# A lower scheduler priority for the position sums and splits of the compressed inputs, in a two-layer hybrid decoder trunk

## The chip, the cores and the metric

The kernel runs on one core of one Trainium2 chip. The metric is the device time of one execution in microseconds (us); the smaller, the better. The core has a TensorE for matmuls (PE in the profile, its weight loads PEld), a VectorE (DVE), a ScalarE (ACT), a GpSimd (POOL) and a SyncE (SP), which here only issues transfers. Each engine works through its own list of instructions in the order in which they were put there, and waits where an operand or a buffer isn't ready.

## The reference: what is computed

Two layers. In each, h = RMSNorm(x) is multiplied by one wide projection W_in. Its columns feed three mixers: a conformer convolution (31 taps, depthwise), a native sparse attention (NSA) with compressed, selected and window branches, and a latent attention (MLA) with four heads. Then come cross attention and a SwiGLU feed-forward. The change stands where the NSA's compressed keys and values are made:

```python
def compress_blocks(tok, pos, w1, b1, w2, n_cmp):
    idx = CMP_STRIDE * jnp.arange(n_cmp)[:, None] + jnp.arange(CMP_BLOCK)[None, :]
    blk = tok[:, idx] + pos[:, None, :]
    blk = blk.transpose(0, 1, 3, 2, 4).reshape(bsz, n_cmp, NSA_KV_GROUPS, CMP_BLOCK * NSA_HEAD_DIM)
    return jax.nn.gelu(blk @ w1 + b1) @ w2
```

There are 31 windows of 32 tokens, stride 16, in two groups of heads, once for the keys (i = 0) and once for the values (i = 1). Everything is 512 tokens by 1024 channels in float32.

## The kernel before

A matrix product in float32 is made from three products of a faster type: each operand is split into a high and a low part, hi = cast(x) on ACT and lo = x - hi on DVE (`hilo`, L93 and L94), and `mm3` (L86, L87, L88) adds hi*hi, lo*hi and hi*lo in a bank of PSUM. So nearly every matrix that PE reads has first passed ACT and DVE.

The instructions aren't listed by hand. The program runs under a scheduler with a modelled clock, which at each point gives an engine the ready instruction with the lowest priority number; that number (`tc.cur_priority`) counts up in the order of the code. A larger number means: later, if anything else is ready. The result is a fixed list for each engine, so on the chip nothing can overtake. The taps of the convolution (`ca`, L587, 120 operations per layer) are written with 100000 added to the number, and fill DVE where nothing else is ready.

The change stands in `mix`, in which the four MLA heads (`head_scores`: scores in `ps_s`, L843 to L847, and the softmax, L852 to L856; `head_mix`: transposes of the probabilities into `ps_t`, L865, their split into `PTh` and `PTl`, then three products a block into `ps_pv`, L878 to L882, and at a head's end the split of the sum, `om`) are interleaved with a filler, `work()`, that takes the other projections step by step. The filler's order in that stretch is: the projection of the compressed keys' input with `windows(p, 0)`; a part of the convolution; two stacked keys interleaved with `compress_in(0)`; the projection of the values' input with `windows(p, 1)`; the first step of `compress_out(0)`; the projection of two query heads (`stacked_queries`); the second step of `compress_out(0)`; and so on with the values, for which `compress_in(1)` reads what `windows(p, 1)` has made.

`windows(p, i)` takes the bank p of the projection. For each of two groups g it adds the position to the even and the odd tokens (L649, two operations of 64x496 from PSUM into `xf`), and splits the sums into `xt` (two casts on ACT and two subtractions on DVE, of 128x248 each). Later `compress_in` uses `xt` as weights of PE (L697, L698).

`compress_out(i)` adds the bias (L705), adds the two halves of the product (L706), and forms the GELU (L707, L708, the tanh on ACT in L709, L710) in a tile `h1`; PE then transposes it (L714). `xf` and `h1` share the tag `gB`, which has one buffer (`bufs` 1). So the first write of `h1` for the keys, L705, can only be made when `xf` of `windows(p, 1)` has been read to the end, by the last two subtractions into `xt`. The tag `ps_t` has two banks, `ps_pv` one, `PTh` and `PTl` have two buffers each, `raw` (weights as loaded) two of 1 MB.

All of this occurs once per layer: `windows(p, 0)` at 97 us and `windows(p, 1)` at 151 us in layer 0, and again in layer 1, where `xf` of `windows(p, 1)` stands at 1089 us.

## Time and profile before

| What | Value |
|---|---|
| Median of 3 runs | 1899.36 us (1898.75 to 1899.78) |
| Profiled execution, its own time | 1898.13 us |
| Its span in the trace | 1896.4 us |
| Granted TensorE clock, mean | 0.999 |
| PE busy | 1877.0 us (99%) |
| DVE busy | 1509.8 us (80%) |
| ACT busy | 1045.7 us (55%) |
| POOL busy | 269.6 us (14%) |
| The four `windows`: L649, 16 operations | 672 ns each |
| Their casts on ACT, 16 | 400 ns each |
| Their subtractions on DVE, 16 | 410 ns each |

The profiled execution is 1.23 us below the median, and its span 1.73 us below its time. A row of a timeline gives the start, the length, the engine, the line, the operation, and the tiles it writes and reads; a bracket at the end is the idle time just before it and what ended that. Rows of one engine overlap a little, since an instruction starts while the one ahead is still writing, so the distance of two starts is what an instruction costs. Matmuls are shown at 0.39 us for 512 columns, and follow each other at 0.23 us.

### The profile page before, as it was taken

What the parts mean: (1) busy time and instruction counts of PE and PEld (TensorE: products, weight loads), DVE (VectorE), ACT (ScalarE), POOL (GpSimd) and SP (SyncE); (2) the same over time, 40 slices, a digit from 0 to 9 for tenths busy, and PEclk for the clock granted to TensorE, in tenths of its full rate; (3) what the DMA queues carried; (4) which work ended last, traced back from release to release, by engine and by line L of the source; (5) the groups of instructions that cost most, each with busy time, mean ns of one, the idle gap of its engine ahead of it and who ended that gap; (6) DMA issues with size and microseconds to landing.
All of it is one profiled execution on the core that took longest, in us unless ns stands there. A gap on an engine that the chain in (4) does not pass through costs nothing.

```text
span 1896.4 us, 29494 instructions
## 1 busy us (share of the span) xinstructions
PE 1877.0 (99%) x10988; PEld 1643.5 (87%) x10988; DVE 1509.8 (80%) x2754; ACT 1045.7 (55%) x1952; POOL 269.6 (14%) x433
## 2 busy tenths in 40 slices
PE   9999999999999999999999999999999999999998
PEld 8887888888887999998888878888888879999986
DVE  7999898764466899998869999986645678999886
ACT  5366557763355645456543765676633465454564
POOL 1211111111122211100022111111112221110000
PEclk9999999999999999999999999999999999999999
DMA  6666554455866666656566665435566766766664
GB/s 188 164 155 185 143 129 127 123 147 157 238 180 161 187 163 186 185 181 197 180 181 164 163 197 129 127 100 136 157 182 177 216 165 159 202 164 163 209 191 159
DMA packets 217644, 318.52 MB, mean 168 GB/s; under 512 B 16352, under 2 KB 153843, under 8 KB 217500
## 3 DMA queue, kind: packets, MB, share of 16 engines
q1 hardware_dynamic: 183116, 216.39, 35.9%
q0 software_dynamic: 31872, 94.39, 23.9%
q10 hardware_dynamic: 2512, 5.85, 0.8%
q8 instruction: 86, 1.41, 0.3%
q14 instruction: 58, 0.48, 0.1%
HBM read 307.13 MB, written 97.54 MB: 213 GB/s over the span
## 4 chain that ended last, share of the span: by engine, by line
PE 87%; DVE 5%; issue 4%; ACT 2%; DMA 1%; POOL 1%; POOLq 0%; SPq 0%; DVEq 0%; ACTq 0%
PE ps_mm L86 14%; PE ps_mm L88 14%; PE ps_mm L87 14%; PE ps_s L86 3%; PE ps_s L88 3%; PE ps_s L87 3%; PE ps_t L86 2%; PE ps_t L87 2%; PE ps_t L88 2%; PE ps_t L1083 2%; PE ps_pv L86 1%; PE ps_pv L88 1%; PE ps_pv L87 1%; PE ps_mm L1374 1%; PE ps_mm L1373 1%
## 5 line engine op out<-in xcount | busy, mean ns | idle before, releaser
L93 ACT CAST wh<-raw 128x1024 fp32r<-128x1024 f32 (+3 forms) x419 | 422.8, 1012 | 498.0 <-PE ps_mm L87 123.5
L94 DVE TENSOR_TENSOR wl<-raw,wh 128x1024 fp32r<-128x1024 f32 (+3 forms) x419 | 488.6, 1172 | 221.6 <-ACT wh L93 218.4
L86 PE MATMUL ps_mm<-hTh,wh 128*128 128x512 f32 (+1 forms) x1152 | 414.6, 360 | 0.5 <-DVE kc L94 0.5
L87 PE MATMUL ps_mm<-hTl,wh 128*128 128x512 f32 (+1 forms) x1152 | 411.2, 357 | 0.0
L88 PE MATMUL ps_mm<-hTh,wl 128*128 128x512 f32 (+1 forms) x1152 | 410.5, 357 | 0.5 <-DVE wl L94 0.5
L88 PEld LDWEIGHTS ps_mm<-hTh,wl 128*128 128x128 f32 x1152 | 217.8, 189 | 32.7 <-DVE wl L94 1.3
L86 PEld LDWEIGHTS ps_mm<-hTh,wh 128*128 128x128 f32 x1152 | 217.9, 189 | 29.4 <-issue 1.3
L87 PEld LDWEIGHTS ps_mm<-hTl,wh 128*128 128x128 f32 x1152 | 217.9, 189 | 26.3 <-issue 0.7
L587 DVE SCALAR_TENSOR_TENSOR ca<-u,vT,ca 128x512 f32<-128x512 f32 x240 | 177.5, 747 | 2.9
L466 POOL DMA_DIRECT2D up<-in_w_gate_up_dram x128 | 85.0, 664 | 538.6 <-PE ps_mm L88 380.9
L466 POOL DMA_DIRECT2D down<-in_w_down_dram x132 | 85.3, 646 | 478.6 <-PE ps_mm L88 255.2
L93 ACT CAST PTh<-ps_t 128x512 fp32r<-128x512 f32 (+4 forms) x136 | 70.6, 519 | 53.2 <-PE ps_t L1083 39.6
L1046 ACT ACTIVATE P<-P,ss 128x512 f32<-128x512 f32 (+3 forms) x128 | 71.6, 560 | 49.2 <-DVE ss L1043 48.2
L86 PE MATMUL ps_s<-rh,wh 128*128 128x256 f32 x320 | 90.6, 283 | 0.0
L87 PE MATMUL ps_s<-rl,wh 128*128 128x256 f32 x320 | 90.6, 283 | 0.0
L88 PE MATMUL ps_s<-rh,wl 128*128 128x256 f32 x320 | 90.6, 283 | 0.0
L94 DVE TENSOR_TENSOR PTl<-ps_t,PTh 128x512 fp32r<-128x512 f32 (+2 forms) x120 | 71.6, 598 | 9.0 <-ACT PTh L93 7.9
L1054 ACT ACTIVATE P<-P,sr 128x512 f32<-128x512 f32 (+3 forms) x128 | 63.3, 555 | 16.9 <-DVE sr L1052 16.8
L86 PE MATMUL ps_mm<-op,wh 128*128 128x512 f32 (+1 forms) x192 | 68.8, 359 | 0.0
L88 PE MATMUL ps_mm<-op,wl 128*128 128x512 f32 (+1 forms) x192 | 68.4, 356 | 0.3
L87 PE MATMUL ps_mm<-op,wh 128*128 128x512 f32 (+1 forms) x192 | 68.0, 355 | 0.0
L86 PEld LDWEIGHTS ps_s<-rh,wh 128*128 128x128 f32 x320 | 61.4, 192 | 0.0
(567 smaller groups left out, 4652.0 us busy)
## 6 DMA issues: line engine op xcount, KB each, us to landing
up<-in_w_gate_up_dram POOLq DMA_DIRECT2D x128, 320.0 KB, 4.4
down<-in_w_down_dram POOLq DMA_DIRECT2D x132, 256.0 KB, 4.3
raw<-in_w_in_dram SPq DMA_DIRECT2D x32, 1024.0 KB
raw<-in_w_gate_up_dram SPq DMA_DIRECT2D x60, 512.0 KB
raw<-up SPq DMA_DIRECT2D x40, 512.0 KB
raw<-down SPq DMA_DIRECT2D x40, 512.0 KB
raw<-in_w_down_dram SPq DMA_DIRECT2D x30, 512.0 KB
raw<-in_w_in_dram SPq DMA_DIRECT2D x26, 512.0 KB
```

The lines of the kernel that those rows point to most:

```text
L86: nc.tensor.matmul(o, lh, rh, start=start, stop=False)
L87: nc.tensor.matmul(o, lh, rl, start=False, stop=False)
L88: tick(nc.tensor.matmul(o, ll, rh, start=False, stop=stop))
L93: nc.scalar.copy(hi, src)
L94: nc.vector.tensor_tensor(lo, src, f(hi), op=OP.subtract)
L466: d = nc.gpsimd.dma_start(dst, src, accum_op=op) if op else nc.gpsimd.dma_start(dst, src)
L587: nc.vector.scalar_tensor_tensor(c, u[:, j:j + T], cw[:, m, j:j + 1], c, op0=OP.mult, op1=OP.add)
L1046: nc.scalar.activation(p[:, c], p[:, c], AF.Exp, bias=s[:, k:k + 1], scale=-1.0, accum_out=s[:, 4 + k:5 + k])
L1054: nc.scalar.activation(P[k], P[k], AF.Copy, scale=r[:, k:k + 1])
L1083: nc.tensor.transpose(tp[:, w:w + 128], P[k][:, j * 128:(j + 1) * 128], ident)
L1373: nc.tensor.matmul(accs[t], xh, u[0][:, k, :], start=j == 0, stop=False)
L1374: nc.tensor.matmul(accs[t], xh, u[1][:, k, :], start=False, stop=False)
```

## The change

Around the loop over the groups in `windows`, the priority number is raised by 50000 and then lowered again:

```diff
             xf = new("gB", (128, 2, 512), name="xf")
+            tc.cur_priority += 50000
             for g in range(2):
                 xv = xf[:, g, 0:496].rearrange("p (k c) -> p k c", k=16)
...
                 for k in range(2):
                     hilo(xt[k][:, :, 0, c], xt[k][:, :, 1, c], xv[:, 8 * k:8 * k + 8])
+            tc.cur_priority -= 50000
             X[i] = xt
```

The adds of L649, the casts and the subtractions into `xt` thus come behind whatever else is ready, and ahead of the taps alone. No operation is added or taken away. Two lines are added, so L649 is L650 in the changed kernel, and lines from L654 on are two higher (L705 is L707, L714 is L716, L881 is L883).

DVE in layer 0 at `windows(p, 1)` before, from the last-but-one subtraction into `xt` (`P` and `s1` belong to the softmax of a head, `wl` to the weights of the next projection, `w1` to the weights of `compress_in(1)`, `op` to stacked operands):

```order
L94 TENSOR_TENSOR xt_1628<-xf_1631,xt_1628 128x8x31
L852 ISA P_1681,s1_1682<-ps_s_1675,mask_823,rst_908 128x256
L852 ISA s1_1682 128x1
L705 TENSOR_TENSOR h1_1644<-ps_mm_1342,b1_1343 62x256
L94 TENSOR_TENSOR wl_1727<-raw_1652,wh_1726 128x1024
L706 TENSOR_TENSOR h1_1644<-h1_1644,ps_mm_1342 62x256
L855 RECIPROCAL s1_1682<-s1_1682 128x1
L94 TENSOR_TENSOR w1_1760<-raw_1761,w1_1760 128x512
L707 TENSOR_TENSOR h1_1644<-h1_1644 62x256
L410 SCALAR_TENSOR_TENSOR op_1706<-ps_mm_1651,op_1706 64x512
L708 SCALAR_TENSOR_TENSOR h1_1644<-h1_1644 62x256
L94 TENSOR_TENSOR PTl_1740<-ps_t_1734,PTh_1739 128x512
```

In this list L705 comes right behind the subtractions, and L710 two rows below this piece.

The same engine and place in the changed kernel, from the last subtractions into `xt` on:

```order
L94 TENSOR_TENSOR xt_1627<-xf_1631,xt_1627 128x8x31
L94 TENSOR_TENSOR om_1806<-ps_pv_1613,om_1805 128x512
L94 TENSOR_TENSOR PTl_1860<-ps_t_1856,PTh_1859 128x256
L94 TENSOR_TENSOR xt_1628<-xf_1631,xt_1628 128x8x31
L587 SCALAR_TENSOR_TENSOR ca_1302<-u_1297,vT_301,ca_1302 128x512
L707 TENSOR_TENSOR h1_1644<-ps_mm_1342,b1_1343 62x256
L94 TENSOR_TENSOR PTl_1911<-ps_t_1906,PTh_1910 128x384
L708 TENSOR_TENSOR h1_1644<-h1_1644,ps_mm_1342 62x256
L94 TENSOR_TENSOR PTl_1982<-ps_t_1976,PTh_1981 128x512
L709 TENSOR_TENSOR h1_1644<-h1_1644 62x256
L587 SCALAR_TENSOR_TENSOR ca_1302<-u_1297,vT_301,ca_1302 128x512
L710 SCALAR_TENSOR_TENSOR h1_1644<-h1_1644 62x256
```

The subtractions into `xt`, and L705 (now L707) with them, have moved behind the split `om_1806` at the end of one head and the first split of the next head (`PTl_1860`); the chain of `h1` is now interleaved with two more of those splits and with taps. L710 (now L712) follows two rows below.

PE in the same place before, from the last products of that head (`pv_1613`) to the projection of the query heads (`ps_mm_1725`):

```order
L846 MATMUL ps_s_1790<-op_590,op_1073 128x512
L847 MATMUL ps_s_1790<-op_591,op_1073 128x512
L880 MATMUL ps_pv_1613<-PTh_1739,op_1147 128x512
L881 MATMUL ps_pv_1613<-PTl_1740,op_1147 128x512
L882 MATMUL ps_pv_1613<-PTh_1739,op_1148 128x512
L714 MATMUL ps_mm_1712<-ident_81,h1_1644 128x62 x2
L86 MATMUL ps_mm_1725<-hTh_135,wh_1726 128x512
L87 MATMUL ps_mm_1725<-hTl_136,wh_1726 128x512
L88 MATMUL ps_mm_1725<-hTh_135,wl_1727 128x512
```

And in the changed kernel, from the last transposes of the next head's first round on:

```order
L867 MATMUL ps_t_1976<-ident_81,P_1607 128x128
L867 MATMUL ps_t_1976<-ident_81,P_1681 128x128
L867 MATMUL ps_t_1976<-ident_81,P_1607 128x128
L867 MATMUL ps_t_1976<-ident_81,P_1541 128x128
L882 MATMUL ps_pv_1875<-PTh_1910,op_1158 128x384
L883 MATMUL ps_pv_1875<-PTl_1911,op_1158 128x384
L884 MATMUL ps_pv_1875<-PTh_1910,op_1159 128x384
L882 MATMUL ps_pv_1875<-PTh_1981,op_1147 128x512
L883 MATMUL ps_pv_1875<-PTl_1982,op_1147 128x512
L884 MATMUL ps_pv_1875<-PTh_1981,op_1148 128x512
L716 MATMUL ps_mm_1712<-ident_81,h1_1644 128x62 x2
L86 MATMUL ps_mm_1725<-hTh_135,wh_1726 128x512
```

The transposes L714 (now L716) have moved behind 26 instructions of the next head (`ps_t_1856`, `ps_s_1863`, `ps_t_1906`, `ps_t_1976` and all products of `ps_pv_1875`); no matmul of a projection stands among those. The same 26 are moved in layer 1.

DVE at `windows(p, 0)` in layer 0 before (`kf` and `op` of MLA's keys and rotary queries):

```order
L410 SCALAR_TENSOR_TENSOR op_1042<-ps_t_1034,op_1042 64x512
L649 TENSOR_TENSOR xf_1082<-ps_mm_928,vT_301 64x496 x2
L94 TENSOR_TENSOR op_1060<-kf_1061,op_1059 128x512
L410 SCALAR_TENSOR_TENSOR op_1070<-ps_t_1065,op_1070 64x512
L94 TENSOR_TENSOR xt_1079<-xf_1082,xt_1079 128x8x31 x2
L649 TENSOR_TENSOR xf_1082<-ps_mm_928,vT_301 64x496 x2
L410 SCALAR_TENSOR_TENSOR op_1073<-ps_t_1065,op_1073 64x512
L94 TENSOR_TENSOR xt_1079<-xf_1082,xt_1079 128x8x31 x2
L94 TENSOR_TENSOR wl_1099<-raw_1095,wh_1098 128x1024
```

And now:

```order
L410 SCALAR_TENSOR_TENSOR op_1042<-ps_t_1034,op_1042 64x512
L650 TENSOR_TENSOR xf_1082<-ps_mm_928,vT_301 64x496
L94 TENSOR_TENSOR wl_1099<-raw_1095,wh_1098 128x1024
L94 TENSOR_TENSOR op_1060<-kf_1061,op_1059 128x512
L410 SCALAR_TENSOR_TENSOR op_1070<-ps_t_1065,op_1070 64x512
L816 TENSOR_TENSOR kf_1116<-ps_pv_1106,rk_997 128x512
L650 TENSOR_TENSOR xf_1082<-ps_mm_928,vT_301 64x496
L410 SCALAR_TENSOR_TENSOR op_1073<-ps_t_1065,op_1073 64x512
L94 TENSOR_TENSOR op_1115<-kf_1116,op_1114 128x512
```

Here one add of L649 (now L650) has stayed, the second stands five rows later, and the splits into `xt` come behind this piece.

## Prediction

> **What bounds the kernel now.** I read the page's busy times, its slices and its chain first, then PE's waits, then the timeline of DVE and PE where the moved work stands.

> ```profile
> span 1896.4 us, 29494 instructions
> PE 1877.0 (99%) x10988; PEld 1643.5 (87%) x10988; DVE 1509.8 (80%) x2754; ACT 1045.7 (55%) x1952; POOL 269.6 (14%) x433
> PEclk9999999999999999999999999999999999999999
> PE 87%; DVE 5%; issue 4%; ACT 2%; DMA 1%; POOL 1%; POOLq 0%; SPq 0%; DVEq 0%; ACTq 0%
> ```

> PE is busy for 99% of the span at the full clock, and holds 87% of the chain that ended last. No operation is added or removed, so time can only come from PE's waits, and only go into new ones. The waits of PE that touch the moved work are few (engine, line waited at, what it waits for, total, times, longest):

> ```profile
> PE ps_pv L881 <- DVE PTl L94: 2.4, 2, 1.2
> PE ps_mm L714 <- DVE h L710: 0.9, 2, 0.4
> PE ps_mm L86 <- DVE kc L94: 0.5, 2, 0.3
> PE ps_t L86 <- DVE op L410: 0.4, 1, 0.4
> ```

> The first two occur once per layer each, at `windows(p, 1)`; the last once, at `windows(p, 0)` of layer 0. This is DVE there in layer 0:

> ```profile
> 150.75 2.05 DVE L649 TENSOR_TENSOR xf<-ps_mm,vT 64x496 f32<-64x496 f32 x3
> 152.72 0.73 DVE L94 TENSOR_TENSOR xt<-xf,xt 128x248 fp32r<-128x248 f32 x2
> 153.47 0.68 DVE L649 TENSOR_TENSOR xf<-ps_mm,vT 64x496 f32<-64x496 f32 x1
> 154.18 0.56 DVE L94 TENSOR_TENSOR PTl<-ps_t,PTh 128x384 fp32r<-128x384 f32 x1
> 154.65 0.73 DVE L94 TENSOR_TENSOR xt<-xf,xt 128x248 fp32r<-128x248 f32 x2
> ...
> 155.71 0.41 DVE L705 TENSOR_TENSOR h<-ps_mm,b 62x256 f32<-62x256 f32 x1
> 156.04 1.21 DVE L94 TENSOR_TENSOR wl<-raw,wh 128x1024 fp32r<-128x1024 f32 x1
> 157.28 0.42 DVE L706 TENSOR_TENSOR h<-h,ps_mm 62x256 f32<-62x256 f32 x1
> ...
> 159.79 0.68 DVE L94 TENSOR_TENSOR PTl<-ps_t,PTh 128x512 fp32r<-128x512 f32 x1
> 160.50 0.69 DVE L410 SCALAR_TENSOR_TENSOR op<-ps_mm,op 64x512 fp32r<-64x512 f32 x1
> 161.22 0.42 DVE L710 SCALAR_TENSOR_TENSOR h<-h 62x256 f32<-62x256 f32 x1
> 161.67 0.35 DVE L852 CUSTOM_DVE_ANT_0 P<-ps_s,mask,rst 128x128 f32<-128x128 f32 x1
> ...
> 161.95 0.69 DVE L94 TENSOR_TENSOR w<-raw,w 128x512 fp32r<-128x512 f32 x1
> 162.55 0.28 DVE L94 TENSOR_TENSOR PTl<-ps_t,PTh 128x128 fp32r<-128x128 f32 x1
> ...
> 163.67 0.69 DVE L94 TENSOR_TENSOR om<-ps_pv,om 128x512 fp32r<-128x512 f32 x1
> 164.27 1.22 DVE L94 TENSOR_TENSOR wl<-raw,wh 128x1024 fp32r<-128x1024 f32 x1
> 165.41 0.16 DVE L855 RECIPROCAL s<-s 128x1 f32<-128x1 f32 x1
> ...
> 167.84 2.32 DVE L587 SCALAR_TENSOR_TENSOR ca<-u,vT,ca 128x512 f32<-128x512 f32 x3
> ...
> 172.21 0.42 DVE L94 TENSOR_TENSOR PTl<-ps_t,PTh 128x256 fp32r<-128x256 f32 x1
> ```

> The reader is to see that DVE is without a gap (no row has a bracket with idle time) from 150.75 to 161.64, where L710 ends: here DVE sets the pace. PE shows the same from its side:

> ```profile
> 158.85 0.49 PE L880 MATMUL ps_pv<-PTh,op 128*128 128x512 f32 x1 [0.19 <-ACT PTh L93]
> 160.52 0.50 PE L881 MATMUL ps_pv<-PTl,op 128*128 128x512 f32 x1 [1.18 <-DVE PTl L94]
> 160.86 0.40 PE L882 MATMUL ps_pv<-PTh,op 128*128 128x512 f32 x1
> 161.69 0.33 PE L714 MATMUL ps_mm<-ident,h 62*128 62x62 f32 x2 [0.44 <-DVE h L710]
> ...
> 169.64 0.44 PE L865 MATMUL ps_t<-ident,P 128*128 128x128 f32 x2
> 169.83 0.42 PE L843 MATMUL ps_s<-op 128*128 128x384 f32 x1
> ...
> 170.79 0.39 PE L878 MATMUL ps_pv<-PTh,op 128*128 128x512 f32 x1
> 171.02 0.22 PE L881 MATMUL ps_pv<-PTl,op 128*128 128x128 f32 x1
> ...
> 171.19 0.33 PE L697 MATMUL ps_mm<-w,xt 128*128 128x256 f32 x1
> ```

> PE waits 1.18 us for a split `PTl` that stands on DVE behind `windows`' work, and 0.44 us for `h1`, which ends the same DVE stretch.

> **windows(p, 1), what comes forward.** The split `PTl` at 159.79 no longer has the L705 to L708 group ahead of it, but has a tap, `w1` and `wl` instead. The new list up to it, from 150.75: four adds 2.6, `wl` 1.14, two `w1` 1.20, a `PTl` 0.47, a softmax step of 256 columns some 0.4, two subtractions 0.73, a reciprocal 0.1, a tap 0.77, L410 0.72 and the split itself 0.68, together 8.8. It ends near 159.6 instead of 160.47, so L881's wait shrinks by some 0.9 us. That alone brings nothing: the next thing that PE must have is `h1`, and what PE gains here it waits out there.

> **windows(p, 1), what goes back.** L705 needs `xf`'s buffer, so it stands behind the last subtraction into `xt`. Against the old list, the new one has these operations more ahead of L710's end, priced by the distance to the next start where the next row is shown: `w1` 0.60, the 128-column softmax step 0.28, `PTl` of 384 and 512 columns 0.47 and 0.71, `om` 0.60, `wl` 1.14; and by the length less 0.07 (the softmax step's overlap) `PTl` of 128 and 256 columns, 0.21 and 0.35, and a reciprocal, 0.09; and four taps at 2.32/3 = 0.77, 3.09. The sum is 7.5 us; without any overlap, by the lengths, it would be 8.1. Nearly all rows overlap, so I take 7.6: L710 ends at 161.64 + 7.6 = 169.2 if DVE has no gap, and L714 starts at 169.3. Taps can't give way, since the list is fixed.

> On PE, 26 instructions of the next head now stand ahead of L714. Their cost by starts: nine transposes at 0.19/2, 0.86; five score products of 384 columns, 0.96 (169.83 to 170.79); the first three products, 0.40 (to 171.19); three of 256 columns at half the 0.23 of 512 (170.79 to 171.02), 0.35; three of 384 at a fifth of that 0.96, 0.58; three of 512 at 0.23, 0.69. That is 3.8 us of work that PE needn't do later. So PE loses 7.6 - 3.8 = 3.8 us per layer, as waiting. It will be in pieces: the chain of transposes, cast, split and products has no projection between it any more, so I expect waits of 0.4 to 1.2 us at the products, `om` and transposes of `ps_pv_1875` (a split takes its place on DVE among `xt` and taps), about 3 us together, and some 2 us at L714.

> What is late next: `kc`, which comes from L714 by way of `hT`, and for which PE waits 0.26 us a layer already (0.5, twice). If DVE, which has then done four taps and a head's splits early, brings it sooner after L714, that much of the delay is absorbed: 3.8 - 0.26 = 3.5. If not, PE, which has fewer products left to fill the time between the two, waits as much again: 3.8 + 0.26 = 4.1. I take 3.6, nearer to the first, since DVE's backlog is what makes `kc` late.

> **Loads and queues.** The moved operations issue no DMA. `wl` at 156.04 comes forward by some 3 us, and frees the buffer of the next weights' load:

> ```profile
> 157.33 0.37 SPq L102 DMA_DIRECT2D raw<-in_w_in_dram  x1
> 162.65 1.05 ACT L93 CAST wh<-raw 128x1024 fp32r<-128x1024 f32 x1
> ```

> Issued at 157.33, it was cast at 162.65 without a wait for it: at most 5.3 us to land. Issued at 153.3, it is there by 158.6, and the cast on ACT is done by 159.8; the `wl` that reads it now stands on DVE at 159.9. It just fits; a microsecond late would be a microsecond more for all behind it, `h1` included. On ACT the load of the next bias comes later, and on SP one load of bias tables passes a small load of weights; both are read long after, so I cost them at nothing. The casts into `xt` move on ACT, which is 55% busy.

> **windows(p, 0).** No wait of PE for this `xt` is in the list above. One wait is touched:

> ```profile
> 101.64 0.69 DVE L410 SCALAR_TENSOR_TENSOR op<-ps_t,op 64x512 fp32r<-64x512 f32 x1
> 102.48 0.47 PE L86 MATMUL ps_t<-wh,op 128*128 128x512 f32 x1 [0.37 <-DVE op L410]
> ```

> Its L410 loses two adds and two subtractions ahead of it (2 x 0.68 + 0.73 = 2.1), and gets a `wl` (1.14) and a `kf` of 128x512 (as `w1`, 0.6 to 0.7): 0.3 us earlier. The gain lies between 0 and 0.37; I take 0.3, in layer 0 alone.

> **The sum.** 2 x 3.6 - 0.3 = +6.9 us on the profiled 1898.13 is 1905.0; that execution is 1.23 us below the median of the runs, 1899.36, so 1906.2 there. A difference of 0.2% (3.8 us) is about what this kernel's measurement can tell from none. Bounds: per layer 7.5 - 3.84 - 0.26 = 3.4 and 8.1 - 3.84 + 0.26 = 4.5, with 0.37 to 0 for `windows(p, 0)`: +6.4 to +9.0, 1905.8 to 1908.4, if the lists run as their rows did. I stay near the lower end since nearly all rows overlap as the priced ones do.

> **Rivals.** (1) The lateness is mostly covered: for less than 3.8 us in all, L714 would have to come by 167.4, that is 1.9 us earlier than the sum, or one layer would have to lose next to nothing. For it speaks that the 0.77 of a tap comes from taps in a row that wait for each other, and may be less beside other work (0.6, as `w1` of the same size, would take 0.7 off), and that small waits left over all of PE's list could swallow some of the delay; against it, that DVE's list is one row of work and that layer 1 waits at the same two lines for the same time. At 1.5 us a layer it would give 2 x 1.5 - 0.3, about 1902.

> (2) Faster: `windows`' operations leave the way of `PTl`, and `h1` comes in time. Then the waits 1.18, 0.44 and 0.19 go in both layers, and 0.37: 4.0 us, 1895.4. It is decided at L714: the 26 moved instructions would end by 160.2 + 3.8 = 164.0, so L710 would have to end there too, only 2.4 us later than before; with `om`, `wl` and four taps ahead of it in the list, 4.8 us by themselves, it can't, unless the trace's stretch is far from typical.

> (3) The clock falls. In a stretch of 8 us PE would be at work for half of the time, where now no wait exceeds 1.2 us and all slices show the full clock. If it were halved over the 3.8 us of matmuls of that stretch, each layer would lose 3.8 more: 1906.2 + 7.6 = 1913.8. Against it: the work doesn't stop for more than some 2 us at once. [...]

> (4) DVE waits in its turn: if its splits of the moved chain come to wait for PE, the 3 us of PE's waits come on top of the 7.6 instead of lying beside it, up to 3 us a layer: 1912.2. Between the splits stand subtractions and taps that fill it, which speaks against.

> (5) The change doesn't do what it says: the lists show that it moves 26 instructions in both layers.

> **Chances.** The forecast's case (+3.8 to +10) 0.64; (1) 0.19; (2) 0.03; (3) 0.06; (4) 0.06; (5) and mixtures near zero 0.02. So slower by over 0.2% 0.76, within 0.2% 0.21, faster 0.03. The range 1901.2 to 1911.8 leaves out (2), (3), (5), half of (4) and a third of (1), 0.2 in all.

> **What would show it.** Right: PE's wait at L716 (L714 before) grows from 0.44 to about 2 us and starts near 169 us; new waits for `PTl` and `om` of the next head; L883's 1.18 falls to a few tenths; the wait at 102.48 shrinks; DVE is without a gap until L712; the same in layer 1. Wrong: L716 before 167 us, no wait there, or a slice in which PEclk falls below 9. The forecast fails most easily if the list of DVE runs faster than the distances that I took, or if PE finds later waits that were there anyway and absorb the delay.

## The result, and the profile after

The changed kernel takes 1913.45 us (median of 6 runs, 1912.57 to 1915.51), against 1899.57 us of the kernel before on the same chip: a ratio of 1.0074, 95% interval 1.0064 to 1.0085, or 13.9 us more. The direction was forecast; the time lies above the range, and within half a microsecond of what the rival on the clock had been priced at, which held a chance of 0.06.

The page after: its span, PE's busy time, the slices of the granted clock, and the chain.

```profile
span 1911.9 us, 29500 instructions
PE 1883.6 (99%) x10988; PEld 1648.1 (86%) x10988; DVE 1511.7 (79%) x2754; ACT 1045.1 (55%) x1952; POOL 269.4 (14%) x433
PEclk9999999999999999999999999999999999999999
PE 84%; DVE 6%; issue 4%; DMA 3%; ACT 2%; POOL 1%; SPq 0%; POOLq 0%; DVEq 0%; ACTq 0%
```

The span has grown by 15.5 us. PE's idle time went from 1896.4 - 1877.0 = 19.4 to 1911.9 - 1883.6 = 28.3 us, 8.9 more; its busy time grew by 6.6 us, though it does the same work. The slices don't show why: a slice is 48 us long, and a digit of 9 stands for anything from 0.9 up. PE's waits come first (line, releaser, total, times, longest):

```profile
PE ps_mm L716 <- DVE h L712: 6.5, 4, 1.8
PE ps_pv L883 <- DVE PTl L94: 2.4, 4, 0.9
PE ps_t L867 <- DVE PTl L94: 2.1, 2, 1.3
...
PE ps_mm L86 <- DVE kc L94: 1.4, 2, 0.7
...
PE ps_pv L880 <- DVE om L94: 0.9, 2, 0.5
```

And in order of time, PE and then DVE of layer 0:

```profile
159.40 0.50 PE L883 MATMUL ps_pv<-PTl,op 128*128 128x512 f32 x1 [0.88 <-DVE PTl L94]
162.49 0.55 PE L867 MATMUL ps_t<-ident,P 128*128 128x128 f32 x3 [1.27 <-DVE PTl L94]
163.51 0.67 PE L880 MATMUL ps_pv<-PTh,op 128*128 128x512 f32 x1 [0.47 <-DVE om L94]
169.82 0.34 PE L716 MATMUL ps_mm<-ident,h 62*128 62x62 f32 x2 [1.58 <-DVE h L712]
...
170.84 0.63 PE L88 MATMUL ps_mm<-hTh,wl 128*128 128x512 f32 x1
171.27 0.63 PE L86 MATMUL ps_mm<-hTh,wh 128*128 128x512 f32 x1
...
182.19 0.50 PE L86 MATMUL ps_mm<-hTh,wh 128*128 128x512 f32 x1 [0.71 <-DVE kc L94]
...
197.60 0.34 PE L716 MATMUL ps_mm<-ident,h 62*128 62x62 f32 x2 [1.58 <-DVE h L712]
```

```profile
159.97 1.23 DVE L94 TENSOR_TENSOR wl<-raw,wh 128x1024 fp32r<-128x1024 f32 x1 [0.35 <-ACT wh L93]
...
166.76 0.69 DVE L94 TENSOR_TENSOR PTl<-ps_t,PTh 128x512 fp32r<-128x512 f32 x1 [0.65 <-ACT PTh L93]
...
169.36 0.41 DVE L712 SCALAR_TENSOR_TENSOR h<-h 62x256 f32<-62x256 f32 x1
...
192.84 1.23 DVE L94 TENSOR_TENSOR wl<-raw,wh 128x1024 fp32r<-128x1024 f32 x1 [1.84 <-ACT wh L93]
```

The keys' `h1` ends on DVE at 169.77, and PE waits 1.58 us for it. But the matmuls behind it follow each other at 0.43 us (170.84, 171.27), where they took 0.23: PE runs at half clock. Windows of 3.41 us show it (window, its length, the busy time of PE, its weight loads, DVE, ACT and POOL, then the granted clock, DMA share and GB/s):

```profile
160.20:163.61 3.41, 1.67 (x11) 1.14 (x10) 3.32 (x7) 2.76 (x9) 0.00 (x0) 1.00 0.00 0
163.61:167.02 3.41, 3.41 (x14) 3.09 (x14) 2.64 (x7) 1.07 (x2) 0.00 (x0) 0.50 0.00 0
167.02:170.44 3.42, 1.71 (x8) 0.85 (x8) 3.41 (x7) 0.66 (x2) 0.42 (x1) 1.00 0.06 19
170.44:173.85 3.41, 3.41 (x10) 2.64 (x9) 3.02 (x9) 1.45 (x5) 0.52 (x1) 0.50 0.22 51
194.33:197.74 3.41, 1.83 (x12) 1.30 (x10) 3.28 (x8) 2.90 (x5) 0.52 (x1) 1.00 1.09 382
197.74:201.15 3.41, 3.41 (x10) 2.63 (x10) 3.24 (x10) 0.82 (x4) 0.00 (x0) 0.50 0.73 238
1112.51:1115.92 3.41, 1.49 (x7) 0.68 (x6) 3.38 (x8) 0.42 (x1) 0.42 (x1) 1.00 0.08 24
1115.92:1119.33 3.41, 3.41 (x10) 2.64 (x10) 3.32 (x10) 1.69 (x5) 0.52 (x1) 0.50 0.07 12
1139.81:1143.22 3.41, 1.91 (x11) 1.31 (x9) 3.25 (x7) 2.50 (x5) 0.52 (x1) 1.00 1.07 372
```

Ahead of PE's last matmul there are four half-clock stretches. Each lasts one window of 3.41 us and follows a window in which PE was busy for 44 to 54% of the time. They start at 163.61, 170.44, 197.74 and 1115.92: the last three come 2, 10 and 279 times 3.413 us after the first. Two windows of 54 and 56%, from 1105.69 and from 1139.81, weren't followed by one. By an estimate from the clock of 0.50, a stretch costs 3.41/2 = 1.7 us if nothing else is waited for; a fourth of the 6.6 us by which PE's busy time grew is 1.65.

The two layers add up from the lists of waits. The transposes of the convolution's statistics (L896 before, L898 after), which lie behind all this in each layer, start at 316.50 and 325.28 in layer 0, and at 1254.38 and 1269.88 in layer 1: layer 0 loses 8.8 us, layer 1 another 6.7. In layer 0 the waits of this stretch went from 0.37 + 0.19 + 1.18 + 0.44 + 0.26 + 0.34 = 2.8 to 0.88 + 1.27 + 0.47 + 1.58 + 0.71 + 1.58 = 6.5 us, 3.7 more; three half-clock windows are 5.1 us. In layer 1 waits added 4.4 us and one half-clock window 1.7; of the 0.6 us left over, 0.3 is a longer wait for `cn`, and the rest isn't placed.

### The profile page after: what moved, and what is told of

Its sections match the earlier page's. It is cut to its first block, busy times and chain, and to the rows that moved or that the text cites. A ratio compares the mean times of both kernels' runs of the same rounds, so it can differ in the third digit from the quotient of the medians.

```text
span 1911.9 us, 29500 instructions
## 1 busy us (share of the span) xinstructions
PE 1883.6 (99%) x10988; PEld 1648.1 (86%) x10988; DVE 1511.7 (79%) x2754; ACT 1045.1 (55%) x1952; POOL 269.4 (14%) x433
## 4 chain that ended last, share of the span: by engine, by line
PE 84%; DVE 6%; issue 4%; DMA 3%; ACT 2%; POOL 1%; SPq 0%; POOLq 0%; DVEq 0%; ACTq 0%
PE ps_mm L86 14%; PE ps_mm L88 14%; PE ps_mm L87 14%; PE ps_s L86 3%; PE ps_s L88 3%; PE ps_s L87 3%; PE ps_t L87 2%; PE ps_t L88 2%; PE ps_t L86 2%; PE ps_t L1085 2%; DMA raw<-in_w_in_dram 2%; PE ps_pv L86 1%; PE ps_pv L87 1%; PE ps_pv L88 1%; PE ps_mm L1376 1%
## 5 line engine op out<-in xcount | busy, mean ns | idle before, releaser
L93 ACT CAST wh<-raw 128x1024 fp32r<-128x1024 f32 (+3 forms) x419 | 422.3, 1011 | 508.9 <-PE ps_mm L87 125.7
L94 DVE TENSOR_TENSOR wl<-raw,wh 128x1024 fp32r<-128x1024 f32 (+3 forms) x419 | 488.8, 1172 | 228.6 <-ACT wh L93 221.5
L86 PE MATMUL ps_mm<-hTh,wh 128*128 128x512 f32 (+1 forms) x1152 | 416.8, 362 | 1.4 <-DVE kc L94 1.4
L86 PEld LDWEIGHTS ps_mm<-hTh,wh 128*128 128x128 f32 x1152 | 219.0, 190 | 30.5 <-DVE kc L94 1.9
L587 DVE SCALAR_TENSOR_TENSOR ca<-u,vT,ca 128x512 f32<-128x512 f32 x240 | 177.5, 748 | 2.9
L93 ACT CAST PTh<-ps_t 128x512 fp32r<-128x512 f32 (+4 forms) x136 | 70.6, 519 | 61.3 <-PE ps_t L1085 41.3
L86 PE MATMUL ps_s<-rh,wh 128*128 128x256 f32 x320 | 90.6, 283 | 0.0
L94 DVE TENSOR_TENSOR PTl<-ps_t,PTh 128x512 fp32r<-128x512 f32 (+2 forms) x120 | 71.5, 598 | 9.6 <-ACT PTh L93 8.2
L86 PE MATMUL ps_mm<-op,wh 128*128 128x512 f32 (+1 forms) x192 | 68.8, 359 | 0.0
L86 PEld LDWEIGHTS ps_s<-rh,wh 128*128 128x128 f32 x320 | 61.4, 192 | 0.0
```

Of the source, the lines that this page charges most:

```text
L86: nc.tensor.matmul(o, lh, rh, start=start, stop=False)
L93: nc.scalar.copy(hi, src)
L94: nc.vector.tensor_tensor(lo, src, f(hi), op=OP.subtract)
L587: nc.vector.scalar_tensor_tensor(c, u[:, j:j + T], cw[:, m, j:j + 1], c, op0=OP.mult, op1=OP.add)
```

## The experiments

Each was timed against the kernel before on the same chip, whose median was 1899.3 to 1899.7 us. A ratio has its 95% interval.

**Which call: win1_only and win0_only.**

```diff
-            tc.cur_priority += 50000
+            tc.cur_priority += 50000 * i          # win1_only
+            tc.cur_priority += 50000 * (1 - i)    # win0_only
...   (the same factor where the number is lowered again)
```

> Only the second call per layer, windows(p, 1), has the lower priority; windows(p, 0) is as before. Theory (the loss is made at windows(p, 1): h1 of the keys waits for xf's buffer, PE's waits there grow, and the clock falls in windows of about 3.4 us that follow a stretch with about half of PE idle): 1912 to 1915 us, a mean clock of 0.994 to 0.996, a wait of about 1.6 us at L716 near 169 us. Rival (windows(p, 0) has a share of it, or both calls are needed): at least 3 us less, below 1910.5.

> Only the first call per layer, windows(p, 0), has the lower priority. Theory: PE's wait of 0.37 us at 102 us in layer 0 goes, and nothing else: 1899.2 us, within 0.5 us of before, clock 0.999. Rival (the first call has a share of the loss): above 1903.

win1_only took 1912.34 us (1.0071, 1.0058 to 1.0084), as its theory has it, with waits at L716 of 6.3 us in all and three half-clock windows in its trace. So the loss is made at `windows(p, 1)`. win0_only took 1897.75 us (0.9990, 0.9981 to 0.9999): the wait at 102 us is gone, and one of 0.47 us at 1042 us with it. That is 1.45 us below the expected 1899.2, and the only version whose interval lies below 1. The two waits are 0.84 of the 1.9 us gained; where the rest comes from isn't shown.

**The shared buffer: h1_elsewhere and h1_elsewhere_before.** The same edit in the changed kernel and in the kernel before:

```diff
-            both = new("gB", (128, 2, 512), name="h1")
+            both = new("P", (128, 2, 256), name="h1")
```

> The change whole, but h1 is taken from the tag P (six buffers of the same size) instead of gB, so that L707 no longer waits until xf is read. Theory (the shared buffer carries the loss): the chain of h1 and the transposes L716 come ahead of the head's products again, no wait at L716 over 0.5 us, clock 0.999, and the time comes back to that of before or 1 to 4 us below it, 1895.5 to 1899.5. Rival (the late xt and DVE's backlog carry the loss, whatever h1 does): 1905 or more.

> The kernel before with h1 taken from the tag P, priorities unchanged. Theory (at this place DVE sets the pace, and h1 behind xf holds PE up in the kernel before too): the waits of 1.18 and 0.44 us per layer at L881 and L714 go or shrink: 1896 to 1898.5. Rival (they are made by DVE's total work there, so another order only moves the wait): within 0.5 us of before, 1899.1 to 1900.1.

h1_elsewhere took 1899.22 us (0.9999, 0.9990 to 1.0007): the loss is gone with the wait for `xf`'s buffer. Its expectation was met in time but not in detail; other waits took the place (h1_elsewhere, PE's waits):

```profile
PE ps_mm L699 <- ACT w L93: 3.5, 2, 1.8
PE ps_mm L86 <- DVE xf L650: 2.7, 2, 1.4
```

The adds, now late, hold the projection's bank, and `w` is cast late. h1_elsewhere_before took 1900.90 us (1.0009, 1.0000 to 1.0018): PE waited 1.70 us at L714 in each layer, and up to 0.86 for `kc` and 1.65 for `w`. The expectation of a gain failed. What its rival says happened, the wait moved, but the time is 0.8 us above the rival's range.

**How far h1 falls back: splits_only.**

```diff
+            # around the loop: 50000 * (1 - i); and in it:
+                    tc.cur_priority += 50000 * i
                     hilo(xt[k][:, :, 0, c], xt[k][:, :, 1, c], xv[:, 8 * k:8 * k + 8])
+                    tc.cur_priority -= 50000 * i
```

> windows(p, 0) as in the change; in windows(p, 1) only the splits into xt have the lower priority, the adds of L649 are as before. h1 still waits for the last split. PE's list has L716 behind 10 instructions of the next head, where the change has 26. Theory (the loss goes with how far h1 falls behind the head's chain): 1902 to 1908 us. Rival (any late split makes the whole loss): 1911 us or more. Second rival (the late adds, which hold the projection's bank, make it): within 1 us of 1898.

1900.21 us (1.0004, 0.9995 to 1.0012), below the theory's range and 2.2 us above the second rival's 1898. L716 behind 10 instructions has no wait over 0.15 us; PE waits 1.06 us at `PTl` and 1.07 for a softmax sum instead, 2.1 us a layer against 1.8 before. Against win0_only, which treats the first call alike, it is some 2.5 us slower, and its trace has half-clock stretches behind windows busy for 43 and 52%. So late splits alone make the smaller part of the loss. That late adds alone don't make the rest is seen in h1_elsewhere, where they are as late as in the change; what is left is `h1` behind the next head's chain.

**The clock apart from the waits: kept_warm.** Idle matmuls in the changed kernel, which fill waits without shortening them (here those of the third head; nine more stand ahead of the values' transposes):

```diff
+                if h == 2 and j == 2:
+                    for _ in range(6):
+                        nc.tensor.matmul(tp[:, 0:128], ones, ones, start=True, stop=True)
+                if h == 2 and j == 0:
+                    for _ in range(2):
+                        nc.tensor.matmul(last[:, 0:128], ones, ones, start=True, stop=True)
```

> The change whole, with idle matmuls (ones times ones, 128x128 float32, into columns of a bank that nothing reads) put where PE waits: six after the first transposes of the third head, two after its last transposes, nine ahead of the transposes of the values' h1, per layer. No wait is shortened by it. Theory (waits that leave PE idle for about half of a window of 3.4 us halve the clock in the next window, 1.7 us each where PE is the bound): the half-clock stretch after the values' L716 wait and the one after the wait for PTl go, the one after the keys' L716 stays: 1909 to 1912 us, clock 0.996 to 0.998. Rival (the half clock has another cause): at least 1913.5 us, and more by the added matmuls, some 2 us.

1910.94 us (1.0057, 1.0044 to 1.0070), with single runs from 1907.32 (mean clock 0.999) to 1912.23 (0.998). In its trace layer 0 has no half-clock window; the windows there, and the row whose start gives that layer's delay:

```profile
157.10:160.50 3.40, 2.53 (x14) 1.83 (x13) 2.97 (x6) 1.68 (x3) 0.29 (x1) 1.00 0.34 119
160.50:163.90 3.40, 2.44 (x19) 2.10 (x18) 3.31 (x8) 2.37 (x8) 0.00 (x0) 1.00 0.00 0
163.90:167.33 3.43, 2.17 (x16) 1.64 (x15) 3.37 (x9) 1.11 (x3) 0.00 (x0) 1.00 0.06 19
```

```profile
321.43 0.63 PE L907 MATMUL ps_mm<-ident,ca 128*128 128x128 f32 x4 [0.85 <-DVE cn L915]
```

PE is busy for 63 to 74% in them. Layer 0 then ends 321.43 - 316.50 = 4.9 us later than before, where the changed kernel lost 8.8: about 3.9 us of that layer's loss were the clock, though PE had 17 more matmuls to do. These take 0.21 us each, 3.6 in all, and the waits left in that stretch are 0.87 + 0.96 + 0.45 + 0.82 + 0.76 = 3.9 us: together 7.5, more than the 6.5 us of waits in the changed kernel. What went is the clock's 5.1 us. Two things differ from the plan: DVE's list has one tap fewer (0.7 us) ahead of the keys' `h1`, and no wait at all is left at the keys' transposes, where a half-clock stretch was expected to stay. In layer 1 the filling missed (a window at 52% was followed by two at half clock), so the median fell only a little, and its interval overlaps that of the changed kernel: the case rests on layer 0 of the trace. It speaks for the theory and against its rival, that the half clock has another cause.

**The second L716: values_chain_first.**

```diff
+            tc.cur_priority -= 3000 * i     # L707 to L712 of compress_out
...
+            tc.cur_priority += 3000 * i
```

> The change whole, with the elementwise chain of the values' h1 3000 ahead in priority. In DVE's list an L410 and the split om now stand behind steps of that chain instead of ahead of them; the keys' chain and PE's list are as in the change. Theory (the second L716 waits 1.6 to 1.8 us per layer because the 26 instructions that used to cover the way from the last load to this h1 are gone, and DVE's list is what it waits for): the wait falls to about 0.9 us, no half-clock stretch follows it: 1909 to 1912 us. Rival (the way from the load sets it, not DVE's list): the wait stays over 1.5 us, 1912.5 to 1914.

1908.29 us (1.0049, 1.0036 to 1.0062), a little below the theory's range. The wait at the values' transposes was 1.52 us in layer 0 and 1.22 in layer 1 (1.58 and 1.76 in the changed kernel): neither the theory's 0.9 nor the rival's 1.5 and more holds in both layers. In the changed kernel ACT waited for the weights, and DVE for ACT (the `wl` at 192.84 above), while the chain's next step, L709, stood behind that `wl` in DVE's list:

```profile
191.76 1.05 ACT L93 CAST wh<-raw 128x1024 fp32r<-128x1024 f32 x1 [3.44 <-DMA raw<-in_w_in_dram]
```

```profile
190.58 0.42 DVE L708 TENSOR_TENSOR h<-h,ps_mm 62x256 f32<-62x256 f32 x1
...
194.82 0.42 DVE L709 TENSOR_TENSOR h<-h 62x256 f32<-62x256 f32 x1
```

L709 reads nothing but `h1`, which L708 had done with at 191.00. So the late load holds up the chain through the list's order, and the edit left this: in its trace DVE waits 2.33 us for the `wh` of the same `wl`, with the chain's third step behind it. What a chain ahead of `wl` would save isn't tested.

Much of the gain is again the clock: the trace has two half-clock windows in place of four. The windows with the values' wait were busy for 64%, and no half clock followed. The other stretch that is gone, the one behind the keys' wait, isn't the edit's doing as far as is known: that window was busy for 63% here, and for 61% in win1_only, which has no such edit.

**Waits made on purpose: stall_values, _8 and _12.** The kernel before, with n = 4, 8 or 12 passes that change nothing:

```diff
+            for _ in range(n * i):
+                nc.vector.tensor_scalar(u[0:nt], u[0:nt], 1.0, 0.0, op0=OP.mult, op1=OP.add)
             nc.scalar.activation(u[0:nt], u[0:nt], AF.Tanh, scale=0.044715 * math.sqrt(2.0 / math.pi))
```

> The kernel before, with four more passes of DVE over u (times 1, plus 0) in the chain of the values' h1, 0.42 us each; PE's order is unchanged, and L714 of the values comes among projections that keep PE busy. Theory (a wait costs itself and, where it takes half of a window, 1.7 us of clock more): a wait of 1.2 to 1.7 us at the second L714 of each layer, so 1902 to 1903 us by the waits alone; half-clock stretches of 3.4 us behind some of them, their starts on one grid of 3.41 us; median 1903.5 to 1906 and single runs some 1.7 us apart. Rival (only an idle time of a whole window halves the clock): 1902 to 1903 us, clock 0.999, no stretch at half clock.

> As stall_values with eight passes in place of four; a pass took 0.28 us. The scheduler now puts 11 instructions of the last head ahead of the values' L714. Theory: with waits that stay near 1 us at separate places, the half clock comes hardly more often than in the kernel before: 1899.5 to 1902.5 us. Rival (every wait of about 1 us costs a half-clock window): 1903 or more.

> Twelve passes, 3.4 us; 13 instructions come ahead. Theory (a wait that fills half of a window of the 3.41 us grid halves the clock for the next window): waits of 1.5 us and more at the values' L714, half-clock stretches behind them with starts on one grid, clock 0.996 to 0.998, 1902 to 1906 us. Rival (the clock only falls after a whole window of idleness): clock 0.999 but for the stretch that also the kernel before has at times, 1901 to 1903 us by the waits alone.

With four passes (0.28 us each, not 0.42) the waits were 1.14 and 0.39 us; 1900.00 us (1.0002, 0.9993 to 1.0011), no half clock behind them (the window of the first was busy for 67%). So these waits don't tell the theories apart. With eight, 1901.02 us (1.0011, 1.0001 to 1.0020): as expected, since the scheduler filled the wait. With twelve, 1909.48 us (1.0051, 1.0037 to 1.0065), above the 1902 to 1906 of the theory:

```profile
192.79:196.21 3.42, 1.75 (x8) 1.09 (x8) 3.36 (x12) 2.13 (x5) 0.00 (x0) 1.00 0.07 20
196.21:199.62 3.41, 3.41 (x10) 2.73 (x9) 3.32 (x9) 1.24 (x4) 0.00 (x0) 0.50 0.50 154
1134.88:1138.29 3.41, 1.51 (x6) 0.89 (x6) 3.35 (x13) 1.68 (x4) 0.00 (x0) 1.00 0.02 5
1138.29:1141.70 3.41, 3.20 (x9) 2.50 (x10) 3.32 (x10) 1.65 (x4) 0.00 (x0) 0.50 0.45 141
```

No wait in these places was longer than 0.9 us: three of 0.54, 0.89 and 0.66 in layer 0, and 0.67, 0.89 and 0.66 in layer 1, which end within 3.1 us. They cost 2.1 and 2.2 us, and 1.7 us of clock each. A third half-clock window, from 162.07, follows the 1.17 and 0.44 us of waits that the kernel before has at `windows(p, 1)`, in a window busy for 49%. This refutes the rival, that only whole idle windows count, and my own expectation of single waits of 1.5 us and more: here three waits of 0.9 us at most, 2.1 and 2.2 us in sum, left the two windows busy for 51 and 44%.

**Versions that try to take the rest away: h1_and_splits, queries_later, kc_first, kc_first_win0.**

```diff
+            # h1_and_splits: splits_only, with h1 from "P"
+            # kc_first: h1_and_splits, and kc_first_win0: win0_only, each with
+                tc.cur_priority -= 3000
                 hilo(kc[:, 0, :, 0:NCMP], kc[:, 1, :, 0:NCMP], ov)
+                tc.cur_priority += 3000
+            # queries_later: win0_only, with += 600 around stack_q in stacked_queries
+            # and += 600 * i around the splits of w in compress_in
```

> As splits_only, and h1 taken from the tag P. With the change whole and h1 there, PE waited 1.39 us per layer for an add of xf, which held the projection's bank, and 1.7 us for a cast of w. Theory: the adds at their old priority take the first of these away: 1899.2 less 2.8, 1896.4 us; it would be the fastest. Rival (DVE's total work sets the pace there, so that the wait comes back at another line): 1898.5 to 1900 us.

> As win0_only, and the stacking of the queries and the splits of compress_in(1)'s weights are 600 later in priority. In DVE's list one L410 then stands behind L710 instead of ahead of it, at the place where PE waited 0.44 us for L710. Theory: that wait falls by 0.35 us per layer, and with 1.45 us instead of 1.8 us of waits close together the half clock behind them gets rare: 1896 to 1897.3 us, the fastest. Rival (the wait moves to another line): 1897.5 to 1898.5 us.

> As h1_and_splits, and the split of kc is 3000 ahead in priority; in DVE's list it stands ahead of wl (1.2 us) and an L410 (0.7 us) instead of behind them. Theory (a list position, no bound by the amount of work): PE's wait of 1.6 and 1.8 us for kc goes, no wait of over 0.5 us replaces it: 1898.2 less 3.2, 1894.5 to 1896 us, clock 0.999. Rival (the wait comes back at the next operand, w or wl, since DVE or a load sets the pace): 1897.5 to 1899 us.

> As win0_only, with the split of kc ahead of an L410. There PE waited 0.23 and 0.26 us for kc. Theory: these go, 0.5 us, within what can be told: 1896.5 to 1898.3 us. Rival (the half clock behind the waits at L883 and L716 comes oftener or rarer with any shift of the list): up to 1.7 us to either side.

| | median us | ratio, interval | PE's waits there, layers 0 and 1 |
|---|---|---|---|
| h1_and_splits | 1898.18 | 0.9996, 0.9987 to 1.0005 | `kc` 1.60, 1.76; `w` 0.86, 1.32; `h1` 0.62, 0.62 |
| queries_later | 1901.05 | 1.0006, 0.9997 to 1.0014 | `PTl` 1.17, 1.18; none at L716 |
| kc_first | 1897.91 | 0.9992, 0.9983 to 1.0001 | `kc` 1.21, 1.20; `w` 2.12, 1.76; `h1` 0.60, 0.60 |
| kc_first_win0 | 1897.88 | 0.9994, 0.9985 to 1.0003 | as win0_only, `kc` 0.17, 0.17 |

The wait for `xf` went, as expected, and came back at `kc`; in kc_first it came back at `w`, for whose cast on ACT PE waited 2.12 and 1.76 us. So only the line changes, as both rivals say; the time of h1_and_splits lies 0.3 us below its rival's range. kc_first_win0 is within the theory's range, but can't be told from win0_only. queries_later took the wait at L716 away, as expected, and was slower than win0_only by 3.3 us, which was not: in its trace a half-clock window follows in both layers, behind windows busy for 57%, with one large wait of 1.17 us, and most of its runs have a mean clock of 0.997. Why they come oftener there than in win0_only stays open.

## Why the prediction was wrong, point by point

**The lists and DVE's pace: right.** L712 was to end at 169.2 and L716 to start at 169.3; they did at 169.77 and 169.82. DVE had two gaps where none was forecast, 0.35 us for `wh` (the load that "just fits") and 0.65 us for `PTh`, which came late from a PE at half clock; that L716 is still only 0.5 us later than forecast is in part luck, since DVE reached the stretch 0.4 us earlier. The new waits are where they were forecast, but smaller: 1.27 us at the transposes and 0.47 at `om`, 1.7 for "about 3 us together", and 1.58 for "some 2 us at L714". The old wait at L883 fell to 0.88, not to a few tenths. The half clock took the time that was missing there.

**windows(p, 0): right in sign.** 0.3 us was taken for layer 0, and the wait of 0.37 went. The account gave layer 1 nothing; a wait of 0.47 us for `wl` at 1041.79 went there.

**The 3.8 us of work that PE needn't do later: mis-sized.** The account took the 26 instructions as time saved later, less at most 0.26 for `kc`. The stretch up to the values' transposes isn't bound by PE's amount of work alone: there PE waited 0.71 for `kc` instead of 0.26, and 1.58 and 1.76 us for the values' `h1`, where it hadn't waited before and the forecast put nothing. From the keys' transposes to the values' it took 28.4 us before and 27.8 now, though PE had 3.8 us less to do: the 26 instructions had covered DVE's list up to that `h1`, in which a `wl` waits for its load. In sum the waits added 3.7 us in layer 0 (forecast 3.6 - 0.3) and 4.4 in layer 1 (3.6), so this alone would have stayed within the range; kept_warm's layer 0, +4.9 with its added matmuls, agrees. (Without half clock PE would have been done sooner in front of L716 and would have waited longer there, so that the waits alone would have been somewhat more than 3.7.)

**The clock: this step failed.** Rival (3) was given 0.06 because "the work doesn't stop for more than some 2 us at once". That was the wrong measure. PE was to be at work for half of an 8 us stretch, which the prediction says itself, and that is what the trace has: the four windows of 3.41 us that are followed by one at half clock were busy for 44 to 54%, though two others, of 54 and 56%, weren't followed by one. It cost 6.6 us of PE's busy time in the profiled execution, four windows at 1.7. The sign that was named for it, a slice with PEclk below 9, couldn't show it: two such windows leave a slice of 48 us at 0.93. That the rival's own price (7.6 us, the stretch's matmuls doubled) came within half a microsecond of the time is luck: the windows hit the projections behind the stretch as much as the stretch itself, one of the four lay largely under a wait for DVE, and the waits were other ones. That the clock falls only at a longer stop, no run shows: no wait of PE in the changed kernel was longer than 1.8 us, and the clock fell four times, at starts on one grid of 3.413 us.

**The cases.** Without the clock's share the time would have been in the range, as kept_warm's fastest run (1907.32) is. Rivals (1) and (2) fell; (4), DVE waiting for PE, came true for 0.65 us. The range ended at 1911.8, below the one case that happened, although its price stood in the text.

## What to carry to other kernels

A lower priority goes to all that waits for the same buffer: before an operation is made late, look at who takes its buffer next, and what stands behind that in PE's list. Where PE is 99% busy, add up its waits by stretches of some 3.4 us and not one by one: here a stretch in which PE was busy for 38 to 57% mostly cost its waits and up to 1.7 us more. Work that is brought forward on PE is only saved later if PE is the bound there too. In a list that can't be overtaken, look for an operation that waits for a load, and for what stands ready behind it.
